# A hybrid decoder step on one core: who turns DeltaNet's keys, queries and values, and mLSTM's keys

## The chip, the cores and the metric

One NeuronCore of a Trainium2 chip runs the whole kernel. The metric is the device time of one execution in microseconds (us), as the median of several runs. A profile of one execution lists every instruction of the engines: TensorE (PE for matmuls, PEld for its weight loads), VectorE (DVE), ScalarE (ACT), GpSimd (POOL) and SyncE (SP), whose queue (SPq) issues every DMA of this kernel.

## The reference, cut to what matters

One layer with sixteen heads of width 128: six mLSTM heads (A), six gated-DeltaNet heads (B) and four HGRN2 heads (C). All their inputs come from one projection of the normalised input, `(1104 tokens x 2048) @ (2048 x 8984)`, in float32; the heads' outputs are normalised, gated and projected back.

```python
proj = jnp.einsum('bld,de->ble', _rmsnorm(x, norm_w), w_in)      # all heads' q, k, v, gates
conv = jax.nn.silu(causal_conv4(concat[bq, bk, bv]))             # DeltaNet only
qb, kb, vb = l2norm(q) * 128 ** -0.5, l2norm(k), v               # per head, over the 128 features
# DeltaNet, per chunk: A = strict_lower(beta * decay * (k k^T)); solve (I + A) [U, W] = [beta v, beta e^G k]
#   S_new = e^G S + (k * e^(Ge - G))^T (U - W S);   o = e^G q S + (decay * q k^T) (U - W S)
# mLSTM, per chunk:  P = exp(D - m) * (q k^T);  num = a q C + P v
#   C_new = a_s C + (w * k)^T v,  n_new = a_s n + sum(w * k),   with k scaled by 128 ** -0.5
out = jnp.einsum('ble,ed->bld', rmsnorm_per_head(h) * w * silu(z), w_out)
```

The tokens are 1024 prompt tokens with 16 learned ones ahead of them, and 8 samples of 8 tokens each with states of their own.

## The kernel before, in words

**Two layouts.** A projection tile comes out of TensorE with 128 features on the partitions and tokens along the row. The convolution, SiLU and the scores `k q^T` want it so. The state updates (`k^T v`), the norm over features and the scaling by a gate per token want tokens on the partitions. Something has to turn 128x128 blocks between the two.

**Halves and tiles.** The tokens are worked in two halves of 512 prompt tokens (`halves`); the first carries 80 more (`NT0`: 64 sample tokens and the 16 learned ones), which form a *small* group of one 80-row block beside the *main* group of four 128-row blocks. In each half the list `ORDER` of heads is walked; a head has four or five projection tiles (k, q, v, for A also o, and z). A tile is 16 blocks of the contraction; each is three matmuls, since a weight is split into a rounded part and a remainder (`whi` by ScalarE, `wlo` by VectorE, `feed_split`), and so is the input. `feed_ahead` asks for raw weights seven pieces ahead and for splits three ahead; each of the three buffer rings has four places. After both halves the output projection runs (`oacc`).

**Who turns what, before.** DeltaNet's k, q and v, after convolution and SiLU (`conv_post`), are turned by TensorE with the identity: `pck` and `pcq` at the start of `gdn_scan`, `pvb` in its `side()`. mLSTM's k is turned the same way (`pk` in `mlstm_scan`). mLSTM's v and o and HGRN2's v go another way already: VectorE's transpose, which turns 32x32 blocks in place, straight from the projection's bank into a row (`turned_evac`); four DMAs that write the row to DRAM so that the blocks land in the other order (`turn_out`, line 806, pieces of 128 bytes); and one DMA that reads it back with tokens on the partitions (`turn_in`, line 813, pieces of 512 bytes). The heads' outputs are turned by the same helpers in `finish`.

**What sets the order.** Each scan is a generator that yields between steps. A planner (`Weave`, `Clock`) keeps estimated times for each engine; after each block of a projection tile `pump` runs those steps whose due time has come, so that the scans' small matmuls stand among the projection's. `ck.last` sets the earliest time that a step's successor may come, to which `LATENCY` (0.4 us) is added: `ck.last = ck.t["T"] + 5.0` leaves 5 us for a DMA. There are four queues: scans (one at a time, in order), finishing (`finish`), `post` (convolutions) and background (`prep_B` prepares the second half's input). `start_head` lets two heads live; at the first tile of the next but one it drains the older head's scan and what stands in the finishing queue. The framework below then places ScalarE's, VectorE's and the queue's instructions by readiness, so these can stand earlier than in the code; TensorE's follow the code's order nearly everywhere. All operations go through one helper, so every engine instruction has line 137 in the profile, and is told by its tile's name.

**Names in the steps below.** `nrm`: sums of squares and their inverse roots. `kn`, `kwall`, `vb`: k normalised, mLSTM's weighted k, weighted v. `pum`: mLSTM's `k^T v`. `nd`: its numerator and denominator. `pst`: its scores. `gt(tag, g)` gives a buffer by tag, one place each, which scans share in turn.

Of the kernel before, what the change touches and what calls it, by code (L numbers as in the profile page):

```python
# [13 lines left out]
P = 128  # L14
# [16 lines left out]
SQ = 32  # L31
# [159 lines left out]
def hybrid_step(ctx, tc, i, o):  # L191
# [238 lines left out]
    DMA(prows[88:92, :], i["hgrn_lower_bounds"][0].rearrange("(e c) -> e c", c=P))  # L430
    gsc = cp.tile([P, 1], F32, name="gsc")
    gbi = cp.tile([P, 1], F32, name="gbi")
    gn = cp.tile([P, 1], F32, name="gn")
    gli = cp.tile([P, 1], F32, name="gli")
    for t in (gsc, gbi, gn, gli):
# [369 lines left out]

    def turn_out(t, name):

        d = dp.tile([NC * NQ, SQ, NQ, SQ], F32, name=name)
        for q in range(NQ):
            DMA(d[:, :, q].rearrange("x j i -> j x i"), t[SQ * q:SQ * (q + 1), 0:HALF].rearrange("p (x i) -> p x i", i=SQ))  # L810
        return d
# [4 lines left out]
    def turned_evac(half, acc, tag, name, small):  # L816
        t = row(tag, name)
        for a, off, cnt in spans(half, acc):
            n = min(cnt, HALF - off)
            V.transpose(t[:, off:off + n], a[:, 0:n])  # L820
            if n < cnt:
                small(t[:, HALF:off + cnt], a[:, n:cnt])
        return t, turn_out(t, scratch_name(name))

# [11 lines left out]
    def finish(half, head, outs, ssq, scale, zs):  # L836
# [132 lines left out]

    def mlstm_scan(half, h, kT, qT, vT, tho, zs, nm, em, st):  # L970
        W = half.width
# [12 lines left out]
        for g in half.groups:  # L984
# [8 lines left out]
            V.tensor_tensor(E[0:n, :, 0:n], E[0:n, :, 0:n], g.psum(pst, n), op=ALU.mult)  # L993
            Es.append(E)
        yield
        for g in half.groups:
            n = g.n
            pk = bank("pk")
            for c in range(g.nt):
                T.transpose(g.psum(pk)[:, c], g.col(kT, c), ident)  # L1000
            kw = kwall[:, g.idx]
            V.tensor_tensor(kw[0:n], g.psum(pk), gate_col(half, g, K_W, h), op=ALU.mult)
            kws.append(kw)
            v1 = gt("2", g, P + 1)
            G.memset(v1[0:n, :, P:P + 1], 1.0)
            if g.small:
                pv = bank("pv")
                T.transpose(g.psum(pv)[:, 0], g.col(vT[0], 0), ident)
                S.copy(v1[0:n, :, 0:P], g.psum(pv))
            else:  # L1010
                turn_in(v1[:, :, 0:P], vT[1])
                og = gt("3", g)
                turn_in(og, tho[1])
            v1s.append(v1)
# [99 lines left out]

    def conv_post(half, U, ei, Cv):
        base = NB * (NS + 3)
# [30 lines left out]
        yield  # L1147
        silu2(Cv[:, 0:W], U[:, 0:W], Cv[:, 0:W])

    def gdn_scan(half, h, ck_, cq, cv, zs, Gb, eG, bb, st):  # L1150
# [6 lines left out]
        nrm = sp.tile([P, 40], F32, tag="nrm", name="nrm", bufs=1)  # L1157
        V.memset(nrm, 1.0)
        pks = []
        for g in gs:  # L1160
            pk, pq = bank("pck"), bank("pcq")
            for c in range(g.nt):
                T.transpose(g.psum(pk)[:, c], g.col(ck_, c), ident)
            for c in range(g.nt):
                T.transpose(g.psum(pq)[:, c], g.col(cq, c), ident)
            for off, src in ((0, pk), (5, pq)):
                for c in range(g.nt):
                    scr = sq("scr", "scrq", bufs=1)
                    S.activation(scr[0:g.n], g.psum(src)[:, c], AF.Square, accum_out=nrm[0:g.n, off + g.at + c:off + g.at + c + 1])
            pks.append(pk)  # L1170
# [7 lines left out]
        for g, pk in zip(gs, pks):  # L1178
            kn = gt("4", g)
            V.tensor_tensor(kn[0:g.n], g.psum(pk), nrm[0:g.n, 20 + g.at:20 + g.at + g.nt].unsqueeze(2).to_broadcast([g.n, g.nt, P]), op=ALU.mult)  # L1180
            kns.append(kn)
# [76 lines left out]
        def side():  # L1258
# [14 lines left out]
            for g, kn in zip(gs, kns):  # L1273
                n = g.n
                pv = bank("pvb")
                for c in range(g.nt):
                    T.transpose(g.psum(pv)[:, c], g.col(cv, c), ident)
                vb = gt("3", g)
                V.tensor_tensor(vb[0:n], g.psum(pv), gate_col(half, g, K_HB, h), op=ALU.mult)
                vbs.append(vb)  # L1280
# [324 lines left out]
    def done_tile(half, name, what, acc):  # L1605
# [13 lines left out]
        elif kind == "A":  # L1619
# [5 lines left out]
            else:  # L1625
                t[what] = evac(half, acc, {"k": "a", "q": "b"}[what], what + "T", scale=KSCALE if what == "k" else None)
                if what == "q":
                    no_meta(half, t[what])
        elif kind == "B":
            weave.drain_queue("post")  # L1630
# [3 lines left out]
            t[what] = row({"k": "c", "q": "d", "v": "f"}[what], "C" + what)  # L1634
            c["posts"].append(weave.add("post", conv_post(half, U, ei, t[what]), lag="V"))
        else:
# [8 lines left out]
        if what == "z":  # L1645
            def scan():
                st = load_state(i[c["st"]], h) if half.first else None
                if kind == "A":
                    yield from mlstm_scan(half, h, t["k"], t["q"], t["v"], t["o"], t["z"], *c["rows"], st)
                elif kind == "B":  # L1650
# [188 lines left out]
```

## Time and profile before

| | |
|---|---|
| median of 3 runs | 2513.55 us (2512.26 to 2516.11) |
| the profiled execution | 2513.66 us, its span from first to last instruction 2512.0 us |
| granted TensorE clock | 0.991 |
| busy: PE, DVE, ACT, POOL | 2441.6, 1428.0, 995.7, 570.6 us |
| DMA: share of 16 engines, bytes | 54.2%, 348 MB on the hardware queue |

How to read it: busy times overlap, since the engines work side by side, and matmuls are pipelined, so a matmul's length includes time in which the next has already begun. A row of a group gives line, engine, operation, output and inputs, count, then busy time and mean length, then the idle time of the engine just before the group's instructions and what ended it. A row of a timeline gives start, length, engine, line, operation and count, and in brackets the idle time before it and its releaser. A row of waits gives who waited for whom: total us, times, longest.

### The profile page before, as it was taken

The numbers are of one execution on the slowest core, as the hardware profiler recorded it, in microseconds if no ns is written. First come the engines' busy times: TensorE is split into PE (matmuls) and PEld (weight loads), VectorE is DVE, ScalarE is ACT, GpSimd is POOL, SyncE is SP. The second block draws the span as 40 slices with busy tenths as digits, with TensorE's granted clock in tenths as the row PEclk, the third lists the DMA queues.
The fourth block names the chain that finished last, engine by engine and source line by source line (L and its number), as shares of the span: only waits on it lengthen the run. The fifth ranks groups of instructions, "written<-read, shape, count | busy, mean of one in ns | idle before, by whom it ended". The sixth has DMA issues, their size and how long they took to land.

```text
span 2512.0 us, 43999 instructions
## 1 busy us (share of the span) xinstructions
PE 2441.6 (97%) x16086; PEld 2181.8 (87%) x16086; DVE 1428.0 (57%) x3002; ACT 995.7 (40%) x2448; POOL 570.6 (23%) x761
## 2 busy tenths in 40 slices
PE   6899999999999999999899999999999999999998
PEld 5898999999999999999787888888888888888886
DVE  7775655765756655556764557554654545323435
ACT  5643434443435333334542434333533334322324
POOL 5332212421213312113330103110321102211301
PEclk8999999999999999999999999999999999999999
DMA  5666665655635454447554445454554558636735
GB/s 129 156 140 149 147 140 125 162 135 130 153 90 140 109 128 121 113 110 192 145 133 113 125 119 144 117 127 107 132 127 115 131 121 261 182 84 197 256 97 184
DMA packets 681044, 350.82 MB, mean 140 GB/s; under 512 B 260004, under 2 KB 622076, under 8 KB 680828
## 3 DMA queue, kind: packets, MB, share of 16 engines
q1 hardware_dynamic: 680828, 348.01, 54.2%
q8 instruction: 126, 2.06, 0.3%
q14 instruction: 90, 0.74, 0.1%
HBM read 285.71 MB, written 62.19 MB: 138 GB/s over the span
## 4 chain that ended last, share of the span: by engine, by line
PE 77%; issue 6%; DMA 5%; DVE 5%; ACT 3%; SPq 2%; POOL 2%; POOLq 0%; DVEq 0%; ACTq 0%
PE acc L137 58%; PE oacc L137 8%; PE pa L137 1%; DVE wlo L137 1%; PE po L137 1%; PE pyy L137 1%; PE pz L137 1%; POOL res L137 1%; PE nd L137 1%; DMA wraw<-in_w_out_dram 1%; DMA wraw<-in_w_in_dram 1%; DMA px<-in_x_prompt_dram 1%; PE pu L137 1%; ACT whi L137 1%; PE poh L137 1%
## 5 line engine op out<-in xcount | busy, mean ns | idle before, releaser
L137 DVE TENSOR_TENSOR wlo<-wraw,whi 128x512 fp32r<-128x512 f32 x720 | 528.8, 738 | 589.7 <-ACT whi L137 561.3
L137 PE MATMUL acc<-hA,whi 128*128 128x288 f32 (+1 forms) x4544 | 822.3, 303 | 12.4 <-ACT whi L137 7.2
L137 ACT CAST whi<-wraw 128x512 fp32r<-128x512 f32 x720 | 441.8, 618 | 915.6 <-PE acc L137 604.5
L137 PE MATMUL acc<-hB,whi 128*128 128x512 f32 x2272 | 722.0, 399 | 5.5 <-ACT whi L137 3.1
L137 PEld LDWEIGHTS acc<-hA,whi 128*128 128x128 f32 x4544 | 676.3, 190 | 19.2 <-ACT whi L137 9.0
L137 PE MATMUL acc<-hA,wlo 128*128 128x288 f32 x2240 | 487.3, 297 | 2.1 <-DVE wlo L137 2.1
L137 PEld LDWEIGHTS acc<-hB,whi 128*128 128x128 f32 x2272 | 412.3, 189 | 86.8 <-ACT whi L137 3.9
L137 PE MATMUL acc<-hB,wlo 128*128 128x512 f32 x1120 | 440.3, 393 | 2.6 <-DVE wlo L137 2.6
L137 PEld LDWEIGHTS acc<-hA,wlo 128*128 128x128 f32 x2240 | 365.5, 189 | 3.2 <-DVE wlo L137 3.2
L137 PE MATMUL oacc<-whi,y 128*128 128x512 f32 x1088 | 343.5, 390 | 0.8 <-ACT whi L137 0.8
L137 PEld LDWEIGHTS acc<-hB,wlo 128*128 128x128 f32 x1120 | 210.4, 188 | 51.3 <-DVE wlo L137 6.4
L137 PEld LDWEIGHTS oacc<-whi,y 128*128 128x128 f32 x1088 | 204.2, 188 | 44.1 <-ACT whi L137 2.0
L137 PE MATMUL oacc<-wlo,y 128*128 128x512 f32 x576 | 224.8, 390 | 1.2 <-DVE wlo L137 1.0
L137 PEld LDWEIGHTS oacc<-wlo,y 128*128 128x128 f32 x576 | 108.1, 188 | 25.3 <-DVE wlo L137 3.1
L137 POOL TENSOR_TENSOR res<-res,fnw 128x512 f32<-128x512 f32 (+1 forms) x34 | 54.3, 1625 | 255.2 <-ACT oscr L137 255.2
L137 POOL TENSOR_TENSOR y<-y,zs 128x592 fp32r<-128x592 f32 (+1 forms) x32 | 45.4, 1418 | 164.5 <-ACT zs L137 143.7
L137 POOL TENSOR_TENSOR qd<-qT,emb 128x512 f32<-128x512 f32 x12 | 18.1, 1511 | 227.7 <-PE po L137 227.7
L137 DVE TENSOR_TENSOR Yt<-Yc,Bb 128x60 f32<-128x60 f32 (+8 forms) x180 | 37.3, 207 | 42.5 <-DMA Bb<-db 37.6
L137 POOL TENSOR_TENSOR hr<-hr,halfneg 128x4 f32<-128x4 f32 (+1 forms) x48 | 45.0, 938 | 58.1 <-DVE hr L137 56.5
L137 POOL TENSOR_TENSOR X<-Ex,hk 128x256 f32<-128x256 f32 (+1 forms) x40 | 39.0, 974 | 64.7 <-PE pa L137 42.5
L137 POOL TENSOR_TENSOR nrm<-nrm,halfneg 128x10 f32<-128x10 f32 x12 | 23.4, 1954 | 130.0 <-DVE nrm L137 130.0
L137 DVE TENSOR_TENSOR Sx<-Sx,lf 128x256 f32<-128x256 f32 (+2 forms) x60 | 40.1, 670 | 17.7 <-ACT Ex L137 16.6
(420 smaller groups left out, 2777.2 us busy)
## 6 DMA issues: line engine op xcount, KB each, us to landing
wraw<-in_w_in_dram SPq DMA_DIRECT2D x564, 256.0 KB
wraw<-in_w_out_dram SPq DMA_DIRECT2D x144, 256.0 KB
y<-y SPq DMA_DIRECT2D x16, 576.0 KB
px<-in_x_prompt_dram SPq DMA_DIRECT2D x32, 256.0 KB
yd<-y SPq DMA_DIRECT2D x128, 64.0 KB
out_dram<-sst SPq DMA_DIRECT2D x16, 512.0 KB
s<-yd SPq DMA_DIRECT2D x32, 256.0 KB
y<-zs SPq DMA_DIRECT2D x32, 256.0 KB
```

Source lines behind the costliest of these rows:

```text
L137: return f(out, *a, **k)
```

## The change

DeltaNet's three rows are turned by VectorE into a new row `uT` as the last step of `conv_post`, and written to DRAM by four DMAs; `gdn_scan` begins with three reads into the buffers `s4`, `s9` and `s3`, then yields with 7 us. The small group stays with TensorE. mLSTM's k is turned by VectorE straight from the projection's bank when its tile is done, and read back in a new step of `mlstm_scan`, together with v and o, with 5 us ahead of the weighting, which now also applies the factor `KSCALE`. Beside it, leads in the planner change (`prep_B`, `finish`), a yield is put ahead of `prep_B`'s and `finish`'s writes, and four parameter columns become one tile.

```diff
-    gsc = cp.tile([P, 1], F32, name="gsc")          # gbi, gn and gli likewise
+    gpar = cp.tile([P, 4], F32, name="gpar")
+    gsc, gbi, gn, gli = (gpar[:, n:n + 1] for n in range(4))
...
 def prep_B():
-            ck.last = ck.t["T"] + 4.0
+            ck.last = ck.t["T"] + 8.0
...
-            ck.last = ck.t["T"] + 6.0
+            ck.last = ck.t["T"] + 10.0
...
             V.tensor_tensor(lo, src, hi, op=ALU.subtract)
+            ck.last += 1.0
+            yield
...
+    def turn_tile(name):
+        return dp.tile([NC * NQ, SQ, NQ, SQ], F32, name=scratch_name(name))
+
+    def turn_row():
+        return sp.tile([P, HALF], F32, tag="uT", name="uT", bufs=1)
+
+    def turn(src, d):
+        t = turn_row()
+        V.transpose(t, src)
+        turn_out(t, d)
+        return d
...
 def finish(half, head, outs, ssq, scale, zs):
         V.transpose(y[:, 0:HALF], hrs[-1].rearrange("p c e -> p (c e)"))
-        d = turn_out(y, scratch_name("yd"))
-        ck.last += 2.0
+        ck.last += 0.5
+        yield
+        d = turn_out(y, turn_tile("yd"))
+        ck.last = ck.t["T"] + 3.0
         yield
...
 def mlstm_scan(...):
+        ck.last += 1.0
+        yield
+        v1m, og = gt("2", half.main, P + 1), gt("3", half.main)
+        turn_in(kwall[:, half.main.idx], dk)
+        turn_in(v1m[:, :, 0:P], vT[1])
+        turn_in(og, tho[1])
+        ck.last = ck.t["T"] + 5.0
         yield
         for g in half.groups:
-            pk = bank("pk")
-            for c in range(g.nt):
-                T.transpose(g.psum(pk)[:, c], g.col(kT, c), ident)
-            kw = kwall[:, g.idx]
-            V.tensor_tensor(kw[0:n], g.psum(pk), gate_col(half, g, K_W, h), op=ALU.mult)
+            kw = pk = kwall[:, g.idx]
+            if g.small:
+                pk = bank("pk")[:, 0:P].unsqueeze(1)
+                T.transpose(pk[0:n, 0], g.col(kT, 0), ident)
+            V.scalar_tensor_tensor(kw[0:n], pk[0:n], 1.0 if g.small else KSCALE, gate_col(half, g, K_W, h), op0=ALU.mult, op1=ALU.mult)
...
 def conv_post(half, U, ei, Cv, turned):
         silu2(Cv[:, 0:W], U[:, 0:W], Cv[:, 0:W])
+        turn(Cv[:, half.base:half.base + HALF], turned)
...
 def gdn_scan(...):
         for g in gs:
-            pk, pq = bank("pck"), bank("pcq")           # four transposes each by TensorE
+            if g.small:
+                ...                                     # one transpose each, as before
+            else:
+                pk, pq, vm = gt("4", g), gt("9", g), gt("3", g)
+                turn_in(pk, dk)
+                turn_in(pq, dq)
+                turn_in(vm, dv)
+                ck.last = ck.t["T"] + 7.0
+                yield
...
-            kn = gt("4", g)
+            kn = gt("4", g) if g.small else pk          # normalised in place
...
-                pv = bank("pvb")                        # four transposes by TensorE
+                if g.small: ...
+                else:
+                    pv = vb = vm                        # weighted in place
...
 def done_tile(half, name, what, acc):                   # mLSTM's k
+                    u, t["dk"] = turn_row(), turn_tile("kd")
+                    for a, off, cnt in spans(half, acc):
+                        n = min(cnt, HALF - off)
+                        V.transpose(u[:, off:off + n], a[:, 0:n])
+                    turn_out(u, t["dk"])
```

More of the change, by code (lines that the diff above doesn't have):

```diff
@@ L804, in evac, with turn_out @@
         return t
-    def turn_out(t, name):
-        d = dp.tile([NC * NQ, SQ, NQ, SQ], F32, name=name)
+    def turn_tile(name):
[7 more added lines that the diff above has]
+        return d
+    def turn_out(t, d):
         for q in range(NQ):
@@ L967, in mask_rows, with mlstm_scan @@
         causal(v, v, fill, strict, reps=NC)
-    def mlstm_scan(half, h, kT, qT, vT, tho, zs, nm, em, st):
+    def mlstm_scan(half, h, kT, qT, vT, tho, zs, nm, em, st, dk):
         W = half.width
@@ L1113, in conv_evac, with conv_post @@
         return U
-    def conv_post(half, U, ei, Cv):
+    def conv_post(half, U, ei, Cv, turned):
         base = NB * (NS + 3)
@@ L1158, in gdn_scan @@
         V.memset(nrm, 1.0)
+        (ck_, dk), (cq, dq), (cv, dv) = ck_, cq, cv
         pks = []
         for g in gs:
-            pk, pq = bank("pck"), bank("pcq")
[L1162 to L1165, printed above, removed]
+            if g.small:
+                pk, pq = (bank(n)[0:g.n, 0:P].unsqueeze(1) for n in ("pck", "pcq"))
+                T.transpose(pk[:, 0], g.col(ck_, 0), ident)
+                T.transpose(pq[:, 0], g.col(cq, 0), ident)
+            else:
[5 more added lines that the diff above has]
+                yield
             for off, src in ((0, pk), (5, pq)):
@@ L1274, in side @@
                 n = g.n
-                pv = bank("pvb")
[L1276 to L1279, printed above, removed]
+                if g.small:
+                    pv = bank("pvb")[0:n, 0:P].unsqueeze(1)
+                    T.transpose(pv[:, 0], g.col(cv, 0), ident)
+                    vb = gt("3", g)
+                else:
+                    pv = vb = vm
+                V.tensor_tensor(vb[0:n], pv, gate_col(half, g, K_HB, h), op=ALU.mult)
                 vbs.append(vb)
@@ L1628, in done_tile @@
                     no_meta(half, t[what])
+                else:
+                    u, t["dk"] = turn_row(), turn_tile("kd")
[3 more added lines that the diff above has]
+                    turn_out(u, t["dk"])
         elif kind == "B":
@@ L1634, in done_tile @@
             t[what] = row({"k": "c", "q": "d", "v": "f"}[what], "C" + what)
-            c["posts"].append(weave.add("post", conv_post(half, U, ei, t[what]), lag="V"))
+            d = turn_tile("cd")
+            c["posts"].append(weave.add("post", conv_post(half, U, ei, t[what], d), lag="V"))
+            t[what] = t[what], d
         else:
@@ L1648, in scan @@
                 if kind == "A":
-                    yield from mlstm_scan(half, h, t["k"], t["q"], t["v"], t["o"], t["z"], *c["rows"], st)
+                    yield from mlstm_scan(half, h, t["k"], t["q"], t["v"], t["o"], t["z"], *c["rows"], st, t["dk"])
                 elif kind == "B":
```

15 lines of the change are left out of this document (4 added, 11 removed).

## The prediction

> **What bounds the kernel now.** I read the page first, then the time by stage, then the waits. The page's head and its engine line:
>
> ```profile
> span 2512.0 us, 43999 instructions
> ...
> PE 2441.6 (97%) x16086; PEld 2181.8 (87%) x16086; DVE 1428.0 (57%) x3002; ACT 995.7 (40%) x2448; POOL 570.6 (23%) x761
> ```
>
> TensorE is busy nearly the whole span and no other engine comes near it. The profiled execution took 2513.66 us, 1.66 us more than its span, and the median of the runs is 2513.55 us; the sum below is made against 2513.66, so it needs no correction beyond 0.1 us. Busy time by stage, first half of the tokens and then the second (columns: stretch, length, busy time of PE, PEld, DVE, ACT and POOL with counts, clock, DMA share, GB/s):
>
> ```profile
> 0.00:1155.00 1155.00, 1107.11 (x8957) 1078.42 (x8958) 728.44 (x1649) 488.75 (x1313) 308.43 (x494) 0.99 0.55 132
> 1240.00:2110.00 870.00, 865.77 (x4891) 714.90 (x4890) 480.60 (x987) 333.97 (x794) 161.64 (x182) 1.00 0.52 132
> ```
>
> In the second half TensorE stands idle for 870.00 - 865.77 = 4.2 us in all, in the first for 48 us, much of that while the first inputs load. The waits say who follows whom (total us, times, longest):
>
> ```profile
> ACT whi L137 <- PE acc L137: 604.5, 331, 9.0
> ```
> ```profile
> SPq L238 <- DVE wlo L137: 548.7, 254, 7.4
> ```
>
> ScalarE, which splits the weights, waits for TensorE to give its buffers back, and the DMA queue waits for VectorE to give back raw ones. The weight stream runs ahead of TensorE, so what delays ScalarE, VectorE or the queue by a few us is taken up there. The kernel ends when TensorE has worked through its instructions.
>
> **What is removed.** Per head and half, four 128x128 transposes each of DeltaNet's keys, queries and values and of mLSTM's keys: 6 heads x 2 halves x 16 = 192. Their groups:
>
> ```profile
> L137 PE MATMUL pcq<-ident,Cq 128*128 128x128 f32 x48 | 7.2, 272 | 0.0
> L137 PE MATMUL pk<-ident,kT 128*128 128x128 f32 x48 | 7.2, 273 | 0.0
> L137 PE MATMUL pck<-ident,Ck 128*128 128x128 f32 x48 | 7.2, 272 | 0.0
> L137 PE MATMUL pvb<-ident,Cv 128*128 128x128 f32 x48 | 7.2, 272 | 0.0
> ```
>
> The 28.8 us busy counts the drain of the last transpose of each block, under which the next projection already starts. What a block costs the stream is the distance between the projection matmuls on its two sides, less the distance they have without it. TensorE's timeline around a DeltaNet head's keys and queries, its values, and an mLSTM head's keys (start, length, line, instruction, count):
>
> ```profile
> 1994.78 0.39 PE L137 MATMUL acc<-hB,wlo 128*128 128x512 f32 x1
> 1995.02 0.60 PE L137 MATMUL pck<-ident,Ck 128*128 128x128 f32 x4
> ...
> 1995.81 0.71 PE L137 MATMUL acc<-hB,whi 128*128 128x512 f32 x2
> 1996.35 0.39 PE L137 MATMUL acc<-hB,wlo 128*128 128x512 f32 x1
> 1996.58 0.62 PE L137 MATMUL acc<-hB,whi 128*128 128x512 f32 x2
> ```
> ```profile
> 2012.28 0.39 PE L137 MATMUL acc<-hB,wlo 128*128 128x512 f32 x1
> ...
> 2012.87 0.71 PE L137 MATMUL acc<-hB,whi 128*128 128x512 f32 x2
> ```
> ```profile
> 2069.30 0.39 PE L137 MATMUL acc<-hB,wlo 128*128 128x512 f32 x1
> ...
> 2069.88 0.71 PE L137 MATMUL acc<-hB,whi 128*128 128x512 f32 x2
> ```
>
> Undisturbed, the next matmul starts 0.23 us after the last (1996.35 to 1996.58). Keys and queries: 1.03 - 0.23 = 0.80 us. Values: 0.59 - 0.23 = 0.36. mLSTM keys: 0.58 - 0.23 = 0.35. Together 1.51 us for a pair of heads in one half, times 12 = **18.1 us** off the bounding engine. The first half's 80-row group keeps its transposes.
>
> A page of the Trainium skill, "TensorE: Matmul & The Clock Gate", Part 4 (PE-mode transpose), gives about 275 ns for a transpose inside a kernel. The 272 ns of the rows agree with it as a duration; as a price in the stream it would make an estimated 192 x 0.275 = 53 us, where the distances above give 18.
>
> **What is added to VectorE.** A block-wise transpose of 512 columns for each of 36 convolution outputs and for 12 key projections. The same operation from SBUF, and from the projection's bank (min/median/max ns):
>
> ```profile
> L137 DVE STREAM_TRANSPOSE y<-s 128x512 f32<-128x512 f32 x32 | 22.6, 707 | 0.5
> ```
> ```profile
> L137 DVE STREAM_TRANSPOSE vT<-acc x18: 370/483/717, 239.9 to 2031.9; 128x288 f32<-128x288 f32 x6, 128x224 f32<-128x224 f32 x6, 128x512 f32<-128x512 f32 x6
> ```
>
> 36 x 0.707 + 6 x 0.717 + 6 x (0.370 + 0.483) = 34.9 us: VectorE goes from 57% to 58%. I cost it at nothing, covered by the up to 9.0 us by which the split weights are ahead; one transpose in front of a weight remainder would cost its 0.7 us without that cover. The scalings of k, q and v stay, now from SBUF, as do the sums of squares on ScalarE.
>
> **What is added to the DMA queue.** 48 x (4 writes + 1 read) = 240 issues. A write's issue (min/median/max ns); the hardware queue over 1968.5 to 1973.5 us, where four such writes of `yd` run with little else; over 1989 to 2009 us, where weights run; and over the page:
>
> ```profile
> L810 SPq DMA_DIRECT2D vT<-vT x48: 303/492/605, 240.7 to 2034.1; - x48
> ```
> ```profile
> q1 hardware_dynamic: 2322, 0.36, 44.8%
> ```
> ```profile
> q1 hardware_dynamic: 3708, 1.84, 37.7%
> ```
> ```profile
> q1 hardware_dynamic: 680828, 348.01, 54.2%
> ```
>
> Packets of 128 bytes take 0.448 x 16 x 5 us / 2322 = 15.4 ns, of 512 bytes 0.377 x 16 x 20 / 3708 = 32.5 ns. One turned row is 2048 of the first on the way out and 512 of the second back: 48.2 us of engine time, 3.0 us on sixteen. Times 48 that is 145 us, and the share goes from 54% to 60%. The queue issues for 240 x 0.49 = 118 us more, and waits on VectorE's transposes and the landing of the writes; behind it stand the weight loads, which the weight stream's lead covers.
>
> **What waits newly.** DeltaNet's scan now begins with three reads and stands 7.4 us in the planner (7.0 and the latency of 0.4). A read of the same shape, from issue to the VectorE instruction that waits for it:
>
> ```profile
> 2070.72 0.37 SPq L814 DMA_DIRECT2D s<-yd  x1
> ```
> ```profile
> 2074.20 0.75 DVE L137 SCALAR_TENSOR_TENSOR y<-s,onw,zs 128x512 f32<-128x512 f32 x1 [0.84 <-DMA s<-yd]
> ```
>
> It lands after 3.5 us. Three in a row, each 512 packets (1.0 us on sixteen engines), land after about 5.5 us: inside 7.4. The values are turned last; the tightest head:
>
> ```profile
> 1873.85 0.69 DVE L137 SCALAR_TENSOR_TENSOR Cv<-U,Cv 128x512 f32<-128x512 f32 x1 [0.78 <-ACT U L137]
> ```
> ```profile
> 1878.73 0.60 PE L137 MATMUL pck<-ident,Ck 128*128 128x128 f32 x4
> ```
>
> From the end of SiLU to the scan's start are 4.2 us; transpose (0.7), four issues (2.0) and landing (taken as the read's 3.5) are 6.2, so the queue may stand 2 us at a head's third read. Bounds 0 and 2 us, hidden again. mLSTM's reads get a step of their own with 5.4 us, but the queue does not follow the code's order closely:
>
> ```profile
> 2060.25 0.43 SPq L814 DMA_DIRECT2D s<-vT  x1
> ```
> ```profile
> 2065.86 1.06 PE L137 MATMUL pst<-qT,kT 128*128 128x128 f32 x8
> ```
>
> The read of v was issued 5.6 us ahead of the scores that precede it in the code; the keys' can be too.
>
> **Where it can cost TensorE.** A DeltaNet head now ends about 7.4 + 1.9 (`finish`'s longer leads) - 1.2 = 8 us later in the plan, and at most two heads are alive: the first tile of the next head but one is followed by a drain that empties the older head's scan and finishing, and what mLSTM steps fall into it stand on TensorE with no projection between them. The trace has three such places, B1, B3 and B5 of the first half; the idle in them, and the extent of the second:
>
> ```profile
> 292.92 0.49 PE L137 MATMUL nd<-s,qd 128*128 128x129 f32 x2 [1.16 <-DVE dn L137]
> ```
> ```profile
> 642.87 0.27 PE L137 MATMUL pot<-ident,tho 128*80 128x128 f32 x1
> ...
> 647.97 0.49 PE L137 MATMUL nd<-s,qd 128*128 128x129 f32 x2 [1.76 <-DVE s L137]
> ...
> 650.48 0.71 PE L137 MATMUL acc<-hA,whi 128*128 128x288 f32 x4
> ```
> ```profile
> 993.74 0.46 PE L137 MATMUL nd<-s,qd 128*128 128x129 f32 x2 [1.38 <-DVE s L137]
> ```
>
> In the second half older head and next head meet to within a us, without idle:
>
> ```profile
> 1788.79 1.05 PE L137 MATMUL pum<-s,kwall 128*128 128x129 f32 x8
> ```
> ```profile
> 1790.33 0.34 SPq L877 DMA_DIRECT2D y<-zs  x1
> ```
> ```profile
> 1790.37 0.38 PE L137 MATMUL nd<-state_A,qd 128*128 128x129 f32 x2
> ```
> ```profile
> 1790.91 0.58 ACT L137 COPY cf<-acc 128x512 f32<-128x512 f32 x1
> ```
>
> Eleven head starts follow a DeltaNet head in this way. Lower bound: nothing. Upper bound without a DMA in it: the three places' mean idle, 1.43 us, at all eleven, 16 us. I take 3 us, two more such places, since the nearest rows (the second half's) show none and mLSTM's own steps also move later, behind the drain.
>
> prep_B's longer leads (4 to 8, 6 to 10) and the merged gate parameters move no instruction of TensorE: nothing. **Sum:** 2513.66 - 18.1 + 3 = 2498.6, so 2499 us.
>
> **The rivals.**
>
> *The drains give most of it back* (no change). All eleven starts get the 1.43 us and the clock or the order costs a little more: 2513.66 - 18.1 + 16 = 2512. For it: the plan is tight at every such start. Against: half of them show no idle today.
>
> *TensorE stands at mLSTM's keys* (slower). If in those drains the weighted keys (`kwall`) come straight from a read that is issued late, `pum` waits in order for landing and scaling, 3.5 + 0.7 us, and `nd` another 1.43: 5.6 us at eleven starts, 62 us, 2513.66 - 18.1 + 62 = 2558. It decides from 18.1 / 11 = 1.6 us a place; half the places give 2527. For it: TensorE takes its instructions in order and a transpose in place needed no landing. Against: the read of v above was issued early.
>
> The Trainium skill, "VectorE: DVE Perf Modes", Rules for kernel authors, sends a full 128x128 transpose to TensorE where a PSUM result will do, which speaks for this rival; the bound of this trace, TensorE at 97% beside VectorE at 57%, speaks against it.
>
> *The whole busy time falls away*: if nothing overlaps the drains of these blocks, 2513.66 - 28.8 = 2485. Against: the starts at 1995.81, 2012.87 and 2069.88 lie under the blocks' ends.
>
> *272 ns each*: 192 x 0.272 = 52 us, 2461. Four transposes in 0.60 us (1995.02) speak against it. It is the case of the 275 ns page of the Trainium skill.
>
> *The change does not do what it says*: the transposes go but TensorE idles as long for another engine, 2513. Against: ScalarE waits 604.5 us for TensorE, not the reverse.
>
> **Chances.** Forecast (2490 to 2508) 0.61; given back 0.14; keys late 0.13; whole busy time 0.08; 272 ns 0.02; idles instead 0.02. Faster by over 0.2% (5 us, about what a measurement tells from no change) is 0.61 + 0.08 + 0.02 = 0.71; within it 0.14 + 0.02 = 0.16; slower 0.13. The range reaches from the whole busy time, 2484, to the edge of no change, 2518, and leaves out 0.15.
>
> **What would show it.** Right: the four groups of 48 gone; TensorE's busy time lower by some 25 to 29 us and its count by 192; the second half shorter by about 9 us; DMA near 60%; idle before `pum`, `kwall` and the sums of squares below 1 us a head; the weight split still waiting for TensorE. Wrong: new stretches without projection of over 3 us at starts of B1, C1, B3, C2, B5 with `kwall` or a turned read as releaser, or ScalarE waiting for reads of the turned rows for longer than 9 us so that `acc` waits for `whi`.

## The result, and the profile after: 2.6% slower

The changed kernel takes 2580.41 us (median of 4 runs, 2576.99 to 2585.97), the kernel before, timed beside it, 2513.27 us (2512.26 to 2516.11). The ratio is 1.0262, 95% interval 1.0245 to 1.0278: 67 us slower, where 14 us faster was forecast. The time lies outside the range of 2484 to 2518. The profiled execution has a span of 2576.4 us, 64.4 above the 2512.0 of before.

The page of the changed kernel, its head, its engine line and the DMA queue:

```profile
span 2576.4 us, 43997 instructions
...
PE 2455.3 (95%) x15894; PEld 2181.9 (85%) x15894; DVE 1452.9 (56%) x3056; ACT 1003.1 (39%) x2452; POOL 569.2 (22%) x761
...
q1 hardware_dynamic: 807548, 373.20, 57.8%
```

The 192 instructions of TensorE are gone (16086 to 15894), VectorE has 25 us more (34.9 were worked out), and the queue's share went from 54.2% to 57.8%. That is near what the prediction had. But TensorE, with less to do, is busy for longer, 2455.3 us after 2441.6, and it also stands more: 2576.4 - 2455.3 = 121.1 us idle, where it was 2512.0 - 2441.6 = 70.4. The cause of the longer busy time is in the view of spans and clocks, of before and of after:

```profile
core 0: 2512.0 us, clock 0.991
```
```profile
core 0: 2576.4 us, clock 0.976
```

(1 - 0.991) x 2512 = 22.6 us were lost to a lower granted clock before, (1 - 0.976) x 2576.4 = 61.8 after. Part of this is counted in the idle time already, since the clock is halved during long stops too, as here (length, TensorE's busy time, clock, DMA share, GB/s):

```profile
789.00:800.00 11.00, 0.00 (x0) 0.50 0.40 80
```

Counted only while TensorE is busy (half of its busy time in the stretches that the trace records at 0.5), the loss is 16.3 us before and 45.3 after. So the account of the 64.4 us is: 50.7 more idle, 29.0 more lost clock, and what is left, 64.4 - 79.7 = -15.3, is what the transposes gave. TensorE's busy time put at full clock spreads by some 5 us either way from kernel to kernel: 2422.8 to 2433.0 us (mean 2427.5) in the eight kernels of this document that keep all 192 transposes, 2409.6 to 2415.8 (mean 2412.1) in the six that drop them. The gain was there, and lost five times over.

By stage, in the two stretches that the prediction shows of before (length, busy time of PE, PEld, DVE, ACT and POOL, clock, DMA share, GB/s):

```profile
0.00:1155.00 1155.00, 1073.34 (x8544) 1040.66 (x8545) 714.64 (x1609) 470.88 (x1257) 289.17 (x478) 0.96 0.59 138
1240.00:2110.00 870.00, 852.28 (x4742) 696.60 (x4741) 496.21 (x1016) 338.15 (x797) 168.01 (x183) 0.98 0.57 137
```

In 1155 us TensorE gets through 8544 instructions instead of 8957, of which the removed transposes explain at most 96. In the second half, where it stood for 4.2 us in all, it now stands for 17.7, at a clock of 0.98 instead of 1.00. The largest loss is in one stretch of the first half, here after and then before:

```profile
784.00:884.00 100.00, 70.97 (x493) 0.83 0.52 120
```
```profile
784.00:884.00 100.00, 100.00 (x806) 1.00 0.47 119
```

TensorE stands for 29.0 us there and loses 6.9 more to the clock while busy: 36 of the 79.7 us within 100 us. Its stops are 14.5 us for the weighted keys, shown below, and two for the weight split:

```profile
PE acc L137 <- ACT whi L137: 13.3, 2, 7.0
```

Ahead of the second of these, at 878 us, ScalarE had stood 5.57 us for VectorE's convolution (`Ck`) before it came to the weight.

Over the whole kernel, TensorE waits for these (total us, times, longest):

```profile
PE acc L137 <- ACT whi L137: 23.4, 11, 7.0
PE pum L137 <- DVE kwall L137: 17.3, 2, 14.5
...
PE pz L137 <- DVE X L137: 8.4, 7, 2.1
...
PE pz L137 <- DVE Yc L137: 4.8, 2, 2.9
```

Of before, the same view has for the first and the last two of these:

```profile
PE acc L137 <- ACT whi L137: 10.3, 9, 3.0
PE pz L137 <- DVE Yc L137: 6.9, 3, 3.6
...
PE pz L137 <- DVE X L137: 1.5, 1, 1.5
```

The wait for the weighted keys did not exist. `pz` waited at the same step under two names, 8.4 us in all before and 13.2 after. ScalarE still waits mostly for TensorE, and the queue for VectorE's remainders, but both less than the 604.5 and 548.7 us of before, the longest wait of the queue now 17.2 us instead of 7.4.

```profile
ACT whi L137 <- PE acc L137: 548.0, 290, 7.0
```
```profile
SPq L238 <- DVE wlo L137: 408.0, 223, 17.2
```

The largest single stop is at the weighted keys, as one of the rivals had it, but once and not at eleven starts. Timeline of the queue, of VectorE and of TensorE around it:

```profile
784.87 0.94 SPq L825 DMA_DIRECT2D kwall<-kd  x1
```
```profile
791.39 0.78 DVE L137 SCALAR_TENSOR_TENSOR hk<-cf,Lr 128x592 f32<-128x592 f32 x1 [3.98 <-ACT Lr L137]
...
796.23 0.74 DVE L137 SCALAR_TENSOR_TENSOR px<-px,bss,pnw 128x512 f32<-128x512 f32 x1
...
799.61 0.69 DVE L137 SCALAR_TENSOR_TENSOR kwall<-kwall,cols 128x512 f32<-128x512 f32 x1
```
```profile
785.56 0.50 PE L137 MATMUL pum<-meta,kwall 80*128 80x137 f32 x2 [0.99 <-DVE ur L137]
800.55 2.06 PE L137 MATMUL pum<-s,kwall 128*128 128x129 f32 x8 [14.49 <-DVE kwall L137]
```

The keys' read is issued only when TensorE is at the step that needs it, and then VectorE has other work in front of the keys: it stands 3.98 us for ScalarE, works mostly on the gates of an HGRN2 head (`hk` and what follows, 791.39 to 796.2), and does prep_B's normalising and one weight split (796.23 to 799.6). After the stop the clock is halved: the eight matmuls of `pum` take 2.06 us here, 1.05 in the row of before at 1788.79.

### The profile page after: what moved, and what is told of

Same layout as the page of the kernel before. It is cut to its first block, busy times and chain, and to the rows that moved or that the text cites. A ratio compares the mean times of both kernels' runs of the same rounds, so it can differ in the third digit from the quotient of the medians.

```text
span 2576.4 us, 43997 instructions
## 1 busy us (share of the span) xinstructions
PE 2455.3 (95%) x15894; PEld 2181.9 (85%) x15894; DVE 1452.9 (56%) x3056; ACT 1003.1 (39%) x2452; POOL 569.2 (22%) x761
## 3 DMA queue, kind: packets, MB, share of 16 engines
q1 hardware_dynamic: 807548, 373.20, 57.8%
## 5 line engine op out<-in xcount | busy, mean ns | idle before, releaser
L137 PE MATMUL acc<-hB,whi 128*128 128x512 f32 x2272 | 729.3, 401 | 9.3 <-DMA hB<-hblo 4.8
L137 PEld LDWEIGHTS acc<-hB,whi 128*128 128x128 f32 x2272 | 419.1, 190 | 94.1 <-DMA hB<-hblo 5.5
L137 ACT ACTIVATE scrq<-s 128x128 f32<-128x128 f32 x224 | 69.2, 309 | 18.7 <-DMA s<-cd 7.9
L137 ACT COPY Wt<-pw 128x128 f32<-128x128 f32 (+1 forms) x54 | 14.4, 266 | 96.9 <-PE pw L137 96.9
```

What stands on the lines that cost most here:

```text
L137: return f(out, *a, **k)
```

## The experiments

In every diff the lines are cut to what matters. The prices are differences between medians that each move by 2 to 5 us from run to run, and the kernel before, timed again with each round, had medians of 2509 to 2513, so a price across rounds is good to some 4 us. Three names recur in the expectations. **Solve** is DeltaNet's triangular solve: its blocks `Ball` go to DRAM (`db`), come back spread out (`Bb`), VectorE works a chain of some thirty small operations (`Yc`, `Yt`) down to `X`, and TensorE's `pz` needs `X`. **Plan** is the order that the kernel's planner writes: a step that it takes to last longer makes the head end later. **Queue** is SyncE's DMA queue, which works in order.

### Which part costs: DeltaNet, mLSTM, or the leads

Four kernels: each half of the change with both longer leads, the whole change with the old leads, and the longer leads alone on the kernel before.

```
e1: conv_post, gdn_scan as changed; mlstm_scan and its keys as before; longer leads
e2: mlstm_scan and its keys as changed; conv_post, gdn_scan as before; longer leads
e3: all as changed, but in prep_B  ck.last = T + 4.0 / + 6.0, no step before the hb writes,
    and in finish  d = turn_out(...); ck.last += 2.0; yield
e4: kernel before, but in prep_B  ck.last = T + 8.0 / + 10.0, += 1.0 and a yield before the hb writes,
    and in finish  ck.last += 0.5; yield; d = turn_out(...); ck.last = T + 3.0; yield
```

> The changed kernel with mLSTM's keys turned by TensorE as before; DeltaNet's rows and all the new leads stay. Keys late (mLSTM's keys read late make pum wait, 17.3 us of idle in two waits, with the half clock behind them some 25 us): about 2550 us. Leads (the longer leads of prep_B push its work into 720 to 884 us, where the stream loses 40 us): still about 2575 us. Load (each of 48 turned rows costs by its DMAs and VectorE time, 36 of 48 stay): about 2513 - 14 + 0.75 x 78, so 2558 us.

> The changed kernel with DeltaNet's keys, queries and values turned by TensorE as before; mLSTM's keys and all the new leads stay. Keys late: the 25 us stay, TensorE saves only 4 us: about 2535 us. Leads: about 2550 us, the 40 us at 784 to 885 us stay. Load: 12 of 48 rows, about 2513 - 4 + 0.25 x 78, so 2529 us.

> The changed kernel with the leads of prep_B and finish as before (4 and 6 us, no extra yields, 2 us ahead of finish's read); all turns by VectorE and DMA stay. Leads: the last of prep_B's writes falls back to about 690 us, the 40 us at 784 to 885 us are gone, about 2535 us. Keys late and load: no change, about 2575 us.

> The kernel before with only the new leads of prep_B (8 and 10 us, a yield ahead of its writes) and of finish (a yield ahead of its writes, 3 us ahead of its read). Leads: slower by 30 to 40 us, about 2550 us, with prep_B's last write near 880 us. Keys late and load: no change from 2513 us beyond 5 us.

| kernel | median us | ratio to before (95%) |
|---|---|---|
| e1, DeltaNet turned | 2564.45 | 1.0211 (1.0176 to 1.0246) |
| e2, mLSTM's keys turned | 2525.42 | 1.0050 (1.0027 to 1.0073) |
| e3, the change with old leads | 2564.33 | 1.0211 (1.0181 to 1.0240) |
| e4, longer leads alone | 2504.05 | 0.9963 (0.9946 to 0.9979) |

None of the three theories of that round had all four. That of a load per turned row came within 6 us in the first two (2558 and 2529) and missed e3 by 11 and e4 by 9. The longer leads, which the changed kernel brings along, are a gain of 7 us by themselves, and against them DeltaNet's turning costs 60 us, mLSTM's 21, both 76. Most of the loss is DeltaNet's, where the prediction's rival had looked for it in mLSTM. The old leads (e3) move the large loss and do not remove it: e3 stands 3.0 us at a clock of 1.00 between 784 and 884 us, but 21.8 us at 0.86 between 655 and 765.

### Is it the step at the head of DeltaNet's scan?

The changed scan begins with three reads and stands 7.0 us in the planner for them. The first kernel has this step and nothing to wait for; the second has the writes and nobody who reads them; the third turns the values alone; the fourth is e1 without the step.

```
e5: e4, and in gdn_scan ahead of the transposes:  ck.last = ck.t["T"] + 7.0; yield
e6: e4, and in conv_post behind SiLU:  turn(Cv[...], "cd")     (nothing reads cd)
e7: e4, only the values turned; vm = gt("3", main); turn_in(vm, ...) behind the reads of Bb
e8: e1, without  ck.last = ck.t["T"] + 7.0; yield  behind the three reads
```

> The longer leads alone ran in 2504 us, with DeltaNet turned too in 2564: 60 us more, and as its 144 transposes would be worth 14 (12 x (0.80 + 0.36)), something costs 74. This kernel has the longer leads and, at the start of DeltaNet's scan, the step of 7.0 us of the changed kernel, with nothing to wait for: TensorE still transposes and nothing is turned. Plan (every head ends 7 us later, so the drains cost): 2504 + 74 = 2578. Queue (the turning's transposes and DMAs cost): 2504. Landing (the scan waits for its reads or their buffers): 2504.

> The longer leads and, behind each convolution, VectorE's transpose and the four writes to DRAM of the changed kernel, 36 x 5 instructions, that nobody reads: TensorE still transposes, and no step is added. Queue: four fifths of the 180 DMAs and all the VectorE work, 2504 + 0.8 x 74 = 2563. Plan: 2504. Landing: 2504, at most 5 more.

> The longer leads and of DeltaNet's three only the values turned; they are read where the scan sends its blocks to DRAM, well ahead of their use, with no step added. Plan: 2504 less the values' transposes (12 x 0.36 = 4): 2500. Queue: a third of the cost, 2504 + 74 / 3 - 4 = 2525. Landing: 2500.

> DeltaNet turned with the longer leads (the kernel that ran in 2564), less the step of 7.0 us after its three reads: the sums of squares are planned right behind them. Plan: 2504 - 14 = 2490. Queue: 2564 as with the step. Landing: ScalarE's sums of squares stand up to 5.5 us at each of the 12 starts, 12 x 5.5 = 66 more than 2564 if nothing covers them: 2564 to 2630.

| kernel | median us | ratio (95%) |
|---|---|---|
| e5, the bare step of 7.0 | 2555.45 | 1.0171 (1.0154 to 1.0189) |
| e6, the writes alone | 2512.39 | 1.0005 (0.9995 to 1.0015) |
| e7, values alone | 2519.97 | 1.0044 (1.0031 to 1.0057) |
| e8, no step | 2551.34 | 1.0166 (1.0146 to 1.0186) |

**The bare step costs 51 us**, with not one transfer and not one instruction of VectorE added. The 144 writes with their 36 transposes on VectorE cost 8. Leaving the step out gives back only 13, since then TensorE does the waiting; 4.04 us at three heads of the first half and 5.04 at three of the second, one row of e8's timeline for them:

```profile
1454.75 1.09 PE L137 MATMUL pkT<-ident,s 128*128 128x128 f32 x4 [5.04 <-DVE s L137]
```

So the time from a read's issue to its use is paid whether the planner knows of it or not. The values alone came out in the middle of what the theories had, 16 above e4; with the writes so cheap, and a step not added, its cost would have to be the read. Which it is was not separated.

Where does a step with nothing in it lose 51 us? The spans, engine lines and clocks of the kernel with the leads alone, and of the one with the step:

```profile
span 2504.7 us, 44000 instructions
...
PE 2444.8 (98%) x16086; PEld 2186.7 (87%) x16086; DVE 1422.9 (57%) x3002; ACT 992.5 (40%) x2448; POOL 570.4 (23%) x761
```
```profile
core 0: 2504.7 us, clock 0.988
```
```profile
span 2554.0 us, 43977 instructions
...
PE 2469.1 (97%) x16086; PEld 2200.1 (86%) x16086; DVE 1427.4 (56%) x3002; ACT 1002.3 (39%) x2454; POOL 570.0 (22%) x761
```
```profile
core 0: 2554.0 us, clock 0.980
```

Idle goes from 59.9 to 84.9 us, the loss to the clock while TensorE is busy from 22.0 to 41.4: 44 of the 49.3 us of the spans. The clock's part may be larger: of e4's seven runs the profiled one had the lowest clock. By the waits of both kernels the idle time is not in the drains themselves: the steps that stand in them, `pum` and `nd`, wait 5.1 us instead of 3.1. One drain, at 1816 us of the kernel with the step, with the mLSTM tail `pk`, `pum`, `nd` run almost without projection, and then the stretch behind a solve (length, TensorE's busy time, clock, DMA share, GB/s):

```profile
1816.00:1824.00 8.00, 7.87 (x49) 1.00 0.65 139
...
1662.00:1676.00 14.00, 14.00 (x102) 0.52 0.34 76
```

In the drain TensorE stands for 0.13 us. At the solve it stands for 3.15, and then works for 14 us at half clock, which loses another 0.48 x 14 = 6.7. The solve of the same head in both kernels, first with the leads alone: the queue, VectorE, TensorE.

```profile
1600.70 5.06 SPq L1214 DMA_DIRECT2D db<-Ball  x8
1605.86 0.53 SPq L238 DMA_DIRECT2D wraw<-in_w_in_dram  x1
...
1607.16 1.92 SPq L1220 DMA_DIRECT2D Bb<-db  x3
```
```profile
1612.07 0.22 DVE L137 TENSOR_TENSOR Yt<-Yc,Bb 128x60 f32<-128x60 f32 x1 [2.69 <-DMA Bb<-db]
...
1620.62 0.31 DVE L137 STREAM_TRANSPOSE X<-Y 128x128 f32<-128x128 f32 x1
```
```profile
1621.02 0.89 PE L137 MATMUL pz<-X,Ball 32*32 32x32 f32 x32
```

Then with the step:

```profile
1636.49 5.59 SPq L1217 DMA_DIRECT2D db<-Ball  x8
...
1642.75 0.50 SPq L785 DMA_DIRECT2D bb<-rows  x1
...
1643.91 1.91 SPq L1223 DMA_DIRECT2D Bb<-db  x3
```
```profile
1650.60 0.22 DVE L137 TENSOR_TENSOR Yt<-Yc,Bb 128x60 f32<-128x60 f32 x1 [5.42 <-DMA Bb<-db]
...
1659.68 0.31 DVE L137 STREAM_TRANSPOSE X<-Y 128x128 f32<-128x128 f32 x1
```
```profile
1660.05 0.89 PE L137 MATMUL pz<-X,Ball 32*32 32x32 f32 x32 [3.15 <-DVE X L137]
```

With the leads alone `X` is done 0.09 us before `pz` starts: at this head the chain has no slack, it just fits. With the step the head sits elsewhere among the others, and another row read (`bb`, 256 KB, beside the `nm` that both have) comes in front of `Bb` on the queue. The chain starts 14.1 us after the blocks began to be sent instead of 11.4: of the 2.74 us, 0.96 pass until `Bb` is issued and 1.78 between its issue and the chain's start. TensorE waits in order. Of the 25.0 us of idle that the step adds, `pz` has 6.3 (4.0 to 10.3), `pkT` behind the normalising 4.6, the start of the output projection (`oacc`) 4.4, `acc` 3.5 behind the weight split and 3.5 behind the DMA of the second half's input, and the drains the 2.0 from above. That the drains bring this about, in that TensorE passes the planner's waits at once and then meets the later steps before the other engines are through, fits the rows but is argued; no run takes a drain away.

### How much per microsecond, and does mLSTM's step cost too?

```
e9:  e2, the four writes of kd issued by nc.gpsimd instead of nc.sync
e10: e5 with 3.5 instead of 7.0
e11: e4, and in mlstm_scan behind the scores:  ck.last += 1.0; yield; ck.last = T + 5.0; yield
e12: the changed kernel with 5.0 instead of 7.0 behind the three reads
```

> mLSTM's keys turned with the longer leads ran in 2525 us, 21 above the longer leads alone. Here the four writes of the turned keys are issued by GpSimd's queue instead of SyncE's; all else stays. Solve (the writes stand on SyncE in front of the blocks that DeltaNet's solve sends to DRAM, TensorE then waits 1.9 to 3.4 us for the solve's X at six places and its clock is halved after it): 2504 less the keys' transposes (12 x 0.35 = 4), 2500. Plan (the two steps added to mLSTM's scan cost): 2525.

> The kernel with the longer leads and the bare step of 7.0 us at DeltaNet's start ran in 2555, 51 above the longer leads alone. Here the step is 3.5 us. Plan (each us by which a head's chain is longer is paid, in proportion): 2504 + 51 / 2 = 2530, 5 either way. Order (any shift only deals the collisions anew): no proportion, anything from 2504 to 2555.

> The longer leads and in mLSTM's scan the two added steps (1.0 and 5.0 us) of the changed kernel, with nothing turned: TensorE transposes the keys as before. Solve (only the writes in front of the solve's blocks cost): 2504. Plan (the steps cost): 2525 + 4 = 2529.

> The changed kernel (2580) with 5.0 instead of 7.0 us after the three reads of DeltaNet's scan. Where no step stood there, ScalarE began the sums of squares 6.0 us after the first read was issued and TensorE waited 4 to 5 us at half of the starts, so 5.0 and the latency of 0.4 nearly cover it. Plan: 2/7 of 51 = 15 less, 2565. Landing (7.0 is needed): the 0.6 us that are not covered at 12 starts, 2580 - 15 + 7 = 2572, or more. Order: no direction.

| kernel | median us | ratio (95%) |
|---|---|---|
| e9, keys turned, their writes by GpSimd | 2512.05 | 1.0007 (0.9995 to 1.0020) |
| e10, bare step of 3.5 | 2530.43 | 1.0077 (1.0061 to 1.0094) |
| e11, mLSTM's bare steps | 2511.19 | 1.0007 (0.9997 to 1.0016) |
| e12, the change with a step of 5.0 | 2567.90 | 1.0233 (1.0214 to 1.0252) |

**The price goes with the length**, as far as two lengths can show it: 0, 3.5 and 7.0 us give 2504, 2530 and 2555. That is 7.3 us for each microsecond, over 12 DeltaNet heads 0.6 us a head. In the changed kernel 2 us less give 12.5 us less where 15 were expected, and only 9.0 when each is taken against the kernel before timed beside it. A step of 6 us in mLSTM's scan costs 7 us in all (9 in that way), not 44: a microsecond has its price at the start of DeltaNet's scan, not everywhere. That any shift only deals the stops anew is made unlikely by this, not excluded.

mLSTM's 21 us are mostly something else. The queue of e2 around a solve, against the 0.53 us of a single weight load between `db` and the row reads in the fence of the leads alone above:

```profile
1429.56 1.99 SPq L821 DMA_DIRECT2D kd<-uT  x4
1431.64 5.63 SPq L1226 DMA_DIRECT2D db<-Ball  x8
1437.37 2.47 SPq L238 DMA_DIRECT2D wraw<-in_w_in_dram  x3
1440.01 1.91 SPq L1232 DMA_DIRECT2D Bb<-db  x3
```
```profile
1453.74 0.89 PE L137 MATMUL pz<-X,Ball 32*32 32x32 f32 x32 [1.91 <-DVE X L137]
```

The turned keys of the next head are written ahead of the solve's blocks, three weight loads instead of one slip in front of the reads, and `X` is late. With the leads alone it was done 2.2 us ahead of `pz` at this head. Five heads of the second half wait like this, for 1.9 to 2.7 us each; over the kernel `pz` waits 14.7 us in e2, 4.0 in e4. With these writes on GpSimd's queue (e9) it waits 6.6, and 13 of the 21 us are gone: 2512, halfway between the forecasts of 2500 and 2525.

### What is left: GpSimd's queue, finish's leads, and whether the prices add up

```
e13: kernel before with prep_B's longer leads only
e14: e12, all 192 writes of turned rows issued by nc.gpsimd
e15: e14, with finish as before
e16: e12, the keys' writes alone issued by nc.gpsimd
e17: e6 with the bare step of e5  (nothing reads cd)
```

> The kernel before (2511) with prep_B's longer leads only; both longer leads ran in 2504. Plan (each us by which a head's chain is longer costs 51 / 7 = 7.3 us over the 12 DeltaNet heads): finish's leads of 1.9 us are the loss and prep_B's the gain, 2504 - 1.9 x 7.3 = 2490. If finish's leads cost nothing, as forecast: 2504. If they were the gain: 2511 or more.

> The changed kernel with the step of 5.0 (2568), all 192 writes of turned rows issued by GpSimd's queue instead of SyncE's. Queue (the writes stand in front of weights, of the solve's blocks and of the weighted keys' read on SyncE): the keys' writes gave 13 back where they were moved alone, DeltaNet's cost 8 alone: 2568 - 21 = 2547. Plan alone: 2568.

> As the run with all writes on GpSimd's queue, and finish's leads as in the kernel before, 1.9 us shorter a head. Plan: 1.9 x 7.3 = 14 below that run, 2533 if that comes to 2547. If finish's leads cost nothing: the same as that run.

> The changed kernel with the step of 5.0 (2568); the four writes of mLSTM's turned keys are issued by GpSimd's queue, DeltaNet's stay on SyncE's. Adding up: 2568 - 13 = 2555. If the single stop of 15.5 us at the weighted keys that this kernel shows in the first half goes too, with the halved clock behind it: some 20 us less, 2548. If the writes were not what held things up: 2568.

> The longer leads, the bare step of 7.0 us at DeltaNet's start and the 144 writes that nobody reads; TensorE still transposes. Adding up: 2555 + 8 = 2563, as much as the kernel with DeltaNet turned (2564), which has 14 us of transposes less, so its 36 reads and what waits for them would cost 15. If step and writes hit harder together, the reads cost nothing and this runs in 2564 + 14 = 2578.

| kernel | median us | ratio (95%) |
|---|---|---|
| e13, prep_B's leads only | 2505.00 | 0.9976 (0.9962 to 0.9989) |
| e14, all writes by GpSimd | 2662.27 | 1.0584 (1.0551 to 1.0617) |
| e15, the same, finish as before | 2662.74 | 1.0603 (1.0559 to 1.0647) |
| e16, the keys' writes by GpSimd | 2595.16 | 1.0329 (1.0306 to 1.0353) |
| e17, step and writes | 2556.88 | 1.0180 (1.0160 to 1.0199) |

e13 and e15 say that finish's longer leads cost nothing and gain nothing, as forecast; the 7.3 us per microsecond hold for the scan, not for the finishing. The gain of e4 is prep_B's.

In the changed kernel with the step of 5.0 GpSimd's queue made things worse, by 94 us with all the writes (e14) and by 27 with the keys' alone (e16), where less time was forecast. GpSimd's timeline in e16, the first and the last of the four writes of one head's keys and what stands behind them:

```profile
1474.81 0.73 POOL L821 DMA_DIRECT2D kd<-uT  x1 [17.42 <-DVE uT L137]
...
1485.88 0.66 POOL L821 DMA_DIRECT2D kd<-uT  x1 [1.89 <-issue]
1486.55 1.98 POOL L137 TENSOR_TENSOR nrm<-nrm,halfneg 128x10 f32<-128x10 f32 x1
```
```profile
1489.31 1.12 PE L137 MATMUL pkT<-ident,s 128*128 128x128 f32 x4 [7.46 <-DVE s L137]
```

From the first to the end of the last it takes 11.7 us, where SyncE's queue issued such a four in 1.99. Behind them waits the power that DeltaNet's normalising needs, and TensorE waits for that. The Trainium skill, "DMA: Bandwidth & Descriptors", Issuing engine by pattern, gives simple loads and stores to SyncE and calls its path generally faster; the 11.7 against 1.99 us agree.

e17 completes an account by runs. Step and writes together cost 53 us, so the writes add 1.5 to the step, not 8. From the kernel before to the changed one, each step a run (medians, us, across rounds):

| step | time | difference | forecast |
|---|---|---|---|
| kernel before | 2511 | | |
| both longer leads (e4) | 2504 | -7 | 0 |
| step of 7.0 at DeltaNet's start (e5) | 2555 | +51 | +3 |
| 36 transposes on VectorE and 144 writes (e17) | 2557 | +2 | 0 |
| 36 reads, less 144 transposes of TensorE (e1) | 2564 | +7 | -14 |
| mLSTM's keys (the changed kernel) | 2580 | +16 | -4 |

The reads, and what waits for them, cost 7 + 14 = 21 us if the transposes are worth what the stream's distances gave. Why was not settled: no run reads without using. Taken against the kernel before timed beside each run, the differences are -7, +53, 0, +7 and +14. They are differences between whole plans, and each plan has its stops at other places: the stretch from 784 to 884 us is the changed kernel's, not e5's. The 16 of the last line holds the single stop of 14.49 us shown above, which e12 has as well (15.53 at the same place) and e16 has not.

The fastest kernels of all are those with prep_B's longer leads and nothing turned, e4 and e13, 2504 to 2505 us: faster than both kernels of this case, by 0.2 to 0.4% against the one before.

## Why the prediction was wrong

**The transposes, 18.1 us: about right.** The account leaves 15, some 5 either way, nearer to the 18.1 of the stream than to the 28.8 of the busy time. The estimate of 53 us by the Trainium skill's 275 ns and the 52 us rival are out.

**VectorE and the writes at nothing: right in size**, 2 us where the step is there already and 8 where it is not. The weight stream covered them, as said.

**The drains at 3 us, bounds 0 and 16: this is the step that failed.** The prediction saw that a DeltaNet head ends about 8 us later in the plan, and then priced this by the idle time that TensorE showed inside three drains of the trace, 1.43 us at each. The bare step measured 51, over three times the upper bound. Two things were mis-sized. The idle was looked for inside the drains, which have 2.0 of the 25.0 us that the step adds; most of it is at `pz`, `pkT`, `acc` and `oacc`, steps later. And the clock was costed at "a little more" in a rival only: it is 19 of the 44 us. The upper bound was taken from rows of the drains. The rows that would have warned are those of before at which `pz` waits for the solve, 8.4 us in four stops: there, and at two heads more, `X` was done less than 0.3 us ahead of its use or too late, and at the other six heads 1.3 to 2.4 us ahead. No term stood for what the changed kernel loses between 784 and 884 us, 36 us in one stretch. No run takes that stretch away alone.

**The reads "inside 7.4": near as a duration, wrong as a cover.** In e8 the squares start 6.0 us after the first issue (5.5 was worked out). But covering a wait by a planned step was itself counted as free.

**The queue at nothing: wrong for mLSTM.** The issues did not fill the queue, which still waits 408.0 us for remainders; what counted was where a few of them stood. Four writes of 1.99 us in front of the solve's blocks cost 13 of e2's 21 us.

**finish's and prep_B's leads at nothing: right for finish, wrong for prep_B**, whose longer leads gain 4 to 7 us in the kernel before. In the changed kernel the old leads were 16 us better (e3); they move the large stops to other places, and why they cost less there is open.

**The rivals.** "TensorE stands at mLSTM's keys" named a place that does occur, and its time of 2558 was the nearest. But its mechanism, 5.6 us at eleven starts, is not what happened: the wait for `kwall` is 17.3 us at two places, the long one is VectorE's other work more than the landing, and DeltaNet alone, with mLSTM as it was, runs in 2564. A number that comes near for another reason is no hit. "The drains give most of it back" had the right cause and a price of 16 instead of 51.

**The signs to look for.** Right: the groups gone, 192 fewer, DMA near 60% (57.8% of a longer span). Right too: the weight split still waits for TensorE. Wrong: TensorE's busy time rose instead of falling by 25 to 29, since half-clock matmuls are counted as busy; the second half, from the first half's last projection to its own, grew from 936 to 954 us instead of shortening by 9; `pum` stood 17.3 us for the keys. `acc` did wait longer for `whi`, but in the stop that ends at 878 us ScalarE had stood for VectorE's convolution, not for a turned read. The sign "new stretches without projection" did appear, and was a poor sign: in the second half they cost next to nothing.

## What to carry to other kernels

Where a planner interleaves a dependent chain with filler, a longer wait in the chain is not free because the filler "covers" it; try it as a bare step, with nothing to wait for, before building what needs the wait. A chain that arrives within 0.1 us of its use has no lead, whatever the average shows: look for the few places where it is waited for, and price what would come in front of that chain on its queue. Count a stop of TensorE with the half-clock stretch behind it: the bare step added 19 us lost to the clock beside 25 us of idle, and at the two short stops whose clock is shown the loss is two and over four times the stop. When adding the two up, count the clock only where TensorE is busy.

## What the runs showed of the hardware that was not expected

Stops much shorter than the stretch of half clock that follows them: in the changed kernel a wait of 1.57 us for `X`, the clock of the stretch behind it, and that of the stretch behind a longer wait at the same step, 2.08 us at 1980.68. From 1385 to 1390 us, ahead of the first wait, the clock was 1.00.

```profile
1394.38 0.89 PE L137 MATMUL pz<-X,Ball 32*32 32x32 f32 x32 [1.57 <-DVE X L137]
```
```profile
1395.00:1410.00 15.00, 15.00 (x121) 0.53 0.25 69
1981.00:1998.00 17.00, 17.00 (x175) 1.00 0.47 112
```

Fifteen microseconds at 0.53 lose 7.0 us for a stop of 1.57. The Trainium skill, "TensorE: Matmul & The Clock Gate", Why this matters for your kernels, asks for no idle gaps of more than about 3 us between bursts. This trace differs: half of that was followed by the half clock here, with small 32x32 matmuls right behind the gap. Not every such stop did it: behind the 2.08 us the clock stayed at 1.00, and in the kernel before `pz` waited 1.48 us in a second half whose clock is 1.00. What decides between them is open.
